# Scan sums in the tile of the turned squares, and the split of the probabilities inside the next keys' group

## Chip, core and metric

The kernel runs on one NeuronCore of a Trainium2 chip, as one launch. The metric is the device time of one execution in microseconds (us), smaller is better. Input and output lie in the chip's memory.

## What is computed

A decoder of two layers over 272 tokens (16 learned meta tokens and 256 tokens of input), width 2048, 16 heads of 128, all in float32. Layer one uses attention with a forget gate, layer two "stick-breaking" attention over keys and values made by `w_kv`. Each layer ends in an MLP of width 8192. The part that the change touches is the attention of layer two:

```python
def stick_breaking_attention(q, k, v):
    scale = HEAD_DIM ** -0.5
    outs = []
    for qs, qe in query_blocks(q.shape[1]):
        z = jnp.einsum('bqhd,bkhd->bhqk', q[:, qs:qe], k[:, :qe]).astype(jnp.float32) * scale
        q_pos = jnp.arange(qs, qe)
        k_pos = jnp.arange(qe)
        mask = k_pos[None, :] < q_pos[:, None]
        log_beta = jax.nn.log_sigmoid(z)
        log_one_minus = jnp.where(mask, jax.nn.log_sigmoid(-z), 0.0)
        suffix = lax.cumsum(log_one_minus, axis=3, reverse=True) - log_one_minus
        a = jnp.where(mask, jnp.exp(log_beta + suffix), 0.0).astype(v.dtype)
        outs.append(jnp.einsum('bhqk,bkhd->bqhd', a, v[:, :qe]))
    return jnp.concatenate(outs, axis=1)
```

The cumulative sum over the keys runs from the last key back; the kernel makes it with a scan.

## The kernel before

**Products.** Activations lie feature-major: 128 features on the partitions, tokens along the free axis. A large product is made by `gemm_group` (L215), which makes 512 output features (four accumulators, m = 0 to 3, of 128) from all 2048 inputs in 192 matmuls. To keep float32 accuracy, each operand is split into a rounded part (hi) and the rest (lo), and three products of parts are added. The weights come from memory in four blocks (kb = 0 to 3), each of two halves; `weights` (L186) loads a half into a tile `raw` (issued by SyncE), ScalarE rounds it to `whi` (L210), and VectorE subtracts to get `wlo` (L211). There are four buffers for halves, so a half can be split only when TensorE has used the one four places earlier. In blocks 0 and 3 the products run accumulator by accumulator over both halves, in blocks 1 and 2 half by half. So a half in the middle serves 24 products. There are four accumulators, and an accumulator is free for the next group when its result has been copied out (for keys and values L480, on VectorE).

**Layer two's attention** (L695 to L777) goes through four groups g of four heads. For each g there is a keys' group (a `gemm_group` with `w_kv[2g]`, L698) and a values' group (`w_kv[2g + 1]`, L743). Beside the values' group the other engines work on the heads in two pairs (pr = 0, 1), L712 to L734:

- the scores z are made on TensorE (L717, L718) and masked (L719); `softplus` (L688 to L693) gives e; a scan on VectorE (L723) gives the sums from the last key back; z minus the sums (L726), then an exponential on ScalarE (L727), gives the probabilities
- `turn_probabilities` (L446) transposes squares of 32 by 32 into a tile `raw` (L451, VectorE) and stores it with four DMAs to `p_dram` (L454, issued by ScalarE)
- `probabilities_back` (L456) reads them back turned, with two DMAs per pair (L461, ScalarE): 512 columns into `raw` and 256 into `p1`
- `split` (L368) rounds the 512 columns on ScalarE (L370) and subtracts on VectorE (L371). The result `p0` (both parts) and `p1` are the moving operands of `weighted` (L423) and L771

In the trace the turned tile and its read-back have the names raw_p, and the split's result the name p. After the values' group, `squares` (L386) turns the values in the same way (L394), `scratch` (L397) stores them with eight DMAs (L401), and `outputs1` (L754) reads them back (L406), splits them (v, L412) and makes the outputs. `outputs1` of group g is called inside the keys' group of g + 1, ahead of its last weight block; for the last group it is called directly.

**Order.** Engines take their instructions in order. DMAs are issued from ScalarE's queue and stand in it between its other instructions. The order of each queue is worked out when the kernel is built (`schedule_with_timeline_sim`, L911). `behind(ins, other)` (L171) adds an ordering without a wait: ins is placed no earlier than other. The list `issued` holds the matmuls of the current group, 0 to 191, so `issued[140]` as a place means behind the 141st product. Before the change the read-backs of the two pairs stand behind products 140 and 176 of the values' group, and both splits behind its last:

```python
        probabilities_back(pps, (140, 176))
        for pr in range(2):
            raw, p0, p1 = pps[pr]
            behind(split(p0.rearrange("p x i q -> p x (i q)"), raw[:, :512]), issued[-1])
```

**Buffers.** Tiles of one tag share its buffers. The tag "pp" has three: for q2 (the split queries, L707 and L708), e, sums and raw of each pair, and turned (the transposed values). p0 of the first pair uses the one buffer of the tag "kT", p0 of the second one of four of "qT", p1 one of two of "relu".

Of the kernel before, what the change touches and what calls it, by code (L numbers as in the profile page):

```python
# [9 lines left out]
F32 = mybir.dt.float32  # L10
# [5 lines left out]
P = 128  # L16
# [17 lines left out]
def yoco_kernel(ctx: ExitStack, tc: tile.TileContext, hT_in, gains, b_f, w_f, w_qkv0, w_o0, w_up, w_dn,  # L34
# [10 lines left out]
    att = ctx.enter_context(tc.tile_pool(name="att", bufs=2))  # L45
# [117 lines left out]
    queued, pinned, issued = [], [False], []  # L163
# [7 lines left out]
    def behind(ins, other):  # L171
        tc.add_manual_dep(ins.ins, other.name, mybir.DependencyInfo(mybir.DependencyClass.NoSync,
                                                                    mybir.DependencyReason.DATA))
# [194 lines left out]
    def split(hl, src):  # L368

        on_act = nc.scalar.activation(hl[:, 0], src, AF.Copy)  # L370
        nc.vector.tensor_tensor(out=hl[:, 1], in0=src, in1=hl[:, 0].bitcast(F32), op=ALU.subtract)  # L371
        return on_act
# [44 lines left out]
    def by_parts(out, a, b, start, stop=False):  # L417

        for k, (i, j) in enumerate(((0, 0), (0, 1), (1, 0))):
            product = nc.tensor.matmul(out, a[i], b[j], start=start and k == 0, stop=stop and k == 2)  # L420
        return product
# [34 lines left out]
    def probabilities_back(pps, places):  # L456
        for pr, at in enumerate(places):
            raw, p0, p1 = pps[pr]
            back = p_dram[pr].rearrange("c j a (h x) -> (c j) (a h) x", h=2)
            for dst, src in ((raw[:, :512], back[:, :, :64]), (p1.rearrange("p i q -> p (i q)"), back[:, :, 64:])):  # L460
                behind(nc.scalar.dma_start(dst.rearrange("p (m x) -> p m x", m=8), src), issued[at])  # L461
# [8 lines left out]
    for g in range(4):  # L470
# [8 lines left out]
        def evac_kv(m, acc, t):  # L479
            nc.vector.tensor_tensor(out=t[:, m, :], in0=acc, in1=box["rstd"], op=ALU.mult)  # L480
# [61 lines left out]
        pps = []  # L542
        for pr in range(2):
            raw = att.tile([P, 2, 2, 256], F32, tag="pp", bufs=3, name=f"raw_p0_{g}_{pr}").rearrange("p x i q -> p (x i q)")
            p0 = att.tile([P, 2, 2, 256], F32R, tag="pp", bufs=3, name=f"p0_{g}_{pr}")
            p1 = tmp.tile([P, T], F32, tag="relu", name=f"p1_{g}_{pr}")[:, :2 * P].rearrange("p (i q) -> p i q", i=2)
# [34 lines left out]
        for pr in range(2):  # L581
            raw, p0, p1 = pps[pr]
# [100 lines left out]
    def backward(a):  # L683

        (step, n), = a.ap[1:]
        return bass.AP(a.tensor, a.offset + (n - 1) * step, [a.ap[0], (-step, n)])
# [9 lines left out]
    for g in range(4):  # L696
        kT = att.tile([P, 4, T], F32, tag="kT", bufs=1, name=f"kT1_{g}")
        gemm_group(w_kv[2 * g], xc, 0, lambda m, acc: evac_kv(m, acc, kT), {3: outputs1} if g else {})  # L698
        q = qT1[g]

        k0 = att.tile([P, 4, T], F32R, tag="vT", bufs=1, name=f"k0_{g}")
        k1 = ao.spare[:, 4 * g:4 * g + 4]
        for j in range(0, 4, 2):
            nc.scalar.activation(k0[:, j:j + 2], kT[:, j:j + 2], AF.Copy)
            nc.vector.tensor_tensor(out=k1[:, j:j + 2], in0=kT[:, j:j + 2], in1=k0[:, j:j + 2].bitcast(F32),
                                    op=ALU.subtract)
        q2 = att.tile([P, 2, 4, P], F32R, tag="pp", bufs=3, name=f"q12_{g}")  # L707
        split(q2, q[:, :, P:S])  # L708
        z = att.tile([P, 4, 416], F32, tag="s", bufs=1, name=f"z_{g}")

        pps = []
        for pr in range(2):  # L712
            zp = z[:, 2 * pr:2 * pr + 2]
            for i in range(2):
                j = 2 * pr + i
                ps = patt.tile([P, 512], F32, tag="patt", name=f"pz_{g}_{j}")
                product = by_parts(ps[:, 144:416], [q2[:, k, j, :] for k in range(2)], [k0[:, j], k1[:, j]], True, True)  # L717
                placed_behind(nc.tensor.matmul(ps[:, 0:144], q[:, j, 0:P], kT[:, j, :144], start=True, stop=True), product)  # L718
                nc.vector.tensor_tensor(out=z[:, j], in0=ps[:, :416], in1=maskB, op=ALU.add)  # L719
            e, sums = (att.tile([P, 2, 2, 256], F32, tag="pp", bufs=3, name=f"{x}_{g}_{pr}")  # L720
                       .rearrange("p x i q -> p (x i q)")[:, :832] for x in ("e", "sums"))
            softplus(e.rearrange("p (i k) -> p i k", i=2), zp)
            nc.vector.tensor_tensor_scan(out=sums, data0=goes_on.rearrange("p i k -> p (i k)"), data1=backward(e), initial=0.0,  # L723
                                         op0=ALU.mult, op1=ALU.add)
            zf = zp.rearrange("p i k -> p (i k)")
            nc.vector.tensor_tensor(out=zf, in0=zf, in1=backward(sums), op=ALU.subtract)  # L726
            nc.scalar.activation(zp, zp, AF.Exp)  # L727

            raw = att.tile([P, 2, 2, 256], F32, tag="pp", bufs=3, name=f"raw_p1_{g}_{pr}").rearrange("p x i q -> p (x i q)")
            p0 = att.tile([P, 4, T], F32R, tag=("kT", "qT")[pr], bufs=(1, 4)[pr], name=f"p01_{g}_{pr}")  # L730
            p0 = p0.rearrange("p h t -> p (h t)")[:, :1024].rearrange("p (x i q) -> p x i q", x=2, i=2)
            p1 = tmp.tile([P, T], F32, tag="relu", name=f"p11_{g}_{pr}")[:, :2 * P].rearrange("p (i q) -> p i q", i=2)
            turn_probabilities(z, raw, pr)
            pps.append((raw, p0, p1))  # L734

        pm = patt.tile([P, 512], F32, tag="patt", name=f"pm1_{g}")
        placed_behind(nc.tensor.transpose(pm[:, 0:P], corners(z[:, :, P:144], z[:, :, 400:416], f"sm1_{g}"), ident), product)
        pm_sb = att.tile([P, 192], F32, tag="pm_sb", bufs=1, name=f"pm_sb1_{g}")
        nc.vector.tensor_tensor(out=pm_sb[:, :P].rearrange("p (b q) -> p b q", q=M), in1=maskD, op=ALU.mult,
                                in0=pm[:, P - M:P].unsqueeze(1).to_broadcast([P, 8, M]))  # L740

        vT = att.tile([P, 4, T], F32, tag="vT", bufs=1, name=f"vT1_{g}")
        gemm_group(w_kv[2 * g + 1], xc, 0, lambda m, acc: evac_kv(m, acc, vT))  # L743
        probabilities_back(pps, (140, 176))
        for pr in range(2):
            raw, p0, p1 = pps[pr]
            behind(split(p0.rearrange("p x i q -> p x (i q)"), raw[:, :512]), issued[-1])


        turned = squares(vT, "pp", f"1_{g}") if g < 3 else None  # L750
        if g < 3:
            scratch(turned, issued[-2:])

        def outputs1(g=g, vT=vT, pps=pps, pm_sb=pm_sb, turned=turned):  # L754
            if turned is not None:
                vs = values_back(turned, issued[64:80:8], issued[112:128:8], f"1_{g}")
            pv = patt.tile([P, 512], F32, tag="patt", name=f"pvc_{g}")
            nc.tensor.transpose(pv[:, :P], corners(vT[:, :, P:144], vT[:, :, 256:T], f"vc1_{g}"), ident)
            vc_sb = att.tile([P, P], F32, tag="vm_sb", bufs=1, name=f"vc_sb_{g}")
            nc.scalar.copy(vc_sb, pv[:, :P])  # L760
            own = att.tile([P, 8, M], F32, tag="own", bufs=1, name=f"own1_{g}")
            for pr in range(2):
                v0, v1 = vs[pr] if turned is not None else token_major(vT, pr, 0, f"1_{g}_{pr}")
                po = patt.tile([P, 2, 256], F32, tag="patt", name=f"po1_{g}_{pr}")
                p0, p1 = in_order(*pps[pr][1:])
                for i in range(2):
                    product = weighted(po, v0, p0, i)
                    if pr == i == 0:
                        placed_behind(nc.tensor.matmul(pv[:, P:2 * P], vc_sb, pm_sb[:, :P], start=True, stop=True), product)
                        nc.scalar.copy(own, pv[:, P:2 * P].rearrange("p (c q) -> p c q", c=8))  # L770
                    nc.tensor.matmul(po[:, i, P:], v1[:, i, :], p1[:, i], start=False, stop=i == 1)  # L771
                ends = po.rearrange("p i (c q) -> p (i c) q", c=2)[:, :, P - M:]
                nc.vector.tensor_tensor(out=ends, in0=ends, in1=own[:, 4 * pr:4 * pr + 4], op=ALU.add)
                put_split(ao, 4 * g + 2 * pr, 2, M, S, po)

        if g == 3:
            outputs1()  # L777
# [141 lines left out]
```

## Time and profile before

| | |
|---|---|
| median of 3 runs | 2306.78 us (2300.99, 2306.78, 2307.44) |
| the profiled execution | 2299.98 us |
| its span, first to last instruction | 2298.2 us |
| mean granted TensorE clock | 0.996 of full speed |
| busy: TensorE, VectorE, ScalarE, GpSimd | 2270.4, 1343.1, 1057.8, 37.9 us |
| memory traffic | 186 GB/s over the span |
| layer two's attention with its keys and values | about 1260 to 1518 us of the span |

How to read the profile: PE is TensorE, PEld its weight loads, DVE VectorE, ACT ScalarE, POOL GpSimd, SP SyncE; "ACTq" marks what ScalarE's sequencer does itself, here DMA issues. L370 is line 370 of the kernel. A row of a timeline has the start in us from the span's start, the duration in us, engine, line, operation, "result<-operands", the shape and the count of merged instructions; a bracket at the end gives the idle time just before and the instruction that ended it. A row of waits has the total in us, the number of waits and the longest. A row of stretches has the stretch and its length, the busy us and counts of PE, PEld, DVE, ACT and POOL, and then the granted clock, the DMA engines' busy share and GB/s. A row of the chain has start, duration, engine, and what ran with how many instructions.

### The profile page before, as it was taken

Reading aid. Unit: us, or ns where it says so; the run is one execution under the profiler, and the core shown is the slowest. Engines: PE = TensorE matmul, PEld = TensorE weight load, DVE = VectorE, ACT = ScalarE, POOL = GpSimd, SP = SyncE. Lnnn points to the kernel's source line nnn. Section 1 sums busy time; section 2 is a strip of 40 time slices with the busy share of each in tenths; the row PEclk is TensorE's granted clock in tenths of the full one; section 3 lists DMA queues with packets and bytes.
Section 4 is the critical chain, followed back from the end, with each engine's and each line's share of the span. In section 5 each row is a group of like instructions: output and inputs, shape, how many; then the busy total and the mean of one; then the engine's idle time right before and its main releaser. Section 6 shows DMA issues by size and latency. Waiting matters only on the chain.

```text
span 2298.2 us, 44896 instructions
## 1 busy us (share of the span) xinstructions
PE 2270.4 (99%) x18830; PEld 2259.3 (98%) x18830; DVE 1343.1 (58%) x1943; ACT 1057.8 (46%) x1451; POOL 37.9 (2%) x78
## 2 busy tenths in 40 slices
PE   9999999999999999999999999999999999999998
PEld 9999999999999999999999989899999999999998
DVE  7766666554554455455566666666555555555555
ACT  6444454453343344344454444455543543543554
POOL 0000000000000000000000000000000000000001
PEclk9999999999999999999999999999999999999999
DMA  7766665555555555555555566656566566565564
GB/s 242 227 196 193 216 183 174 184 174 183 168 187 179 171 187 175 182 168 187 179 178 191 173 180 193 183 184 202 185 192 202 184 201 196 190 201 185 189 205 138
DMA packets 167418, 431.46 MB, mean 188 GB/s; under 512 B 48800, under 2 KB 65072, under 8 KB 167216
## 3 DMA queue, kind: packets, MB, share of 16 engines
q1 hardware_dynamic: 113760, 406.29, 54.8%
q10 hardware_dynamic: 53456, 22.31, 3.9%
q8 instruction: 147, 2.41, 0.4%
q14 instruction: 55, 0.45, 0.1%
HBM read 416.99 MB, written 11.55 MB: 186 GB/s over the span
## 4 chain that ended last, share of the span: by engine, by line
PE 92%; DMA 3%; DVE 2%; issue 1%; ACTq 1%; ACT 1%; POOL 0%; SPq 0%; POOLq 0%; DVEq 0%
PE acc L177 90%; DMA p_dram<-raw_p 1%; DMA raw_p<-p_dram 1%; DVE wlo L211 1%; PE po L420 0%; ACT whi L210 0%; ACTq L454 0%; DMA p<-p_dram 0%; DVE sums L723 0%; DVE z L726 0%; PE ps L420 0%; PE pz L420 0%; DMA v_dram<-turned 0%; DVE raw_p L451 0%; ACTq L461 0%
## 5 line engine op out<-in xcount | busy, mean ns | idle before, releaser
L211 DVE TENSOR_TENSOR wlo<-raw,whi 128x1024 fp32r<-128x1024 f32 (+1 forms) x773 | 927.3, 1216 | 694.6 <-ACT whi L210 687.7
L210 ACT ACTIVATE whi<-raw 128x1024 fp32r<-128x1024 f32 (+1 forms) x773 | 796.0, 1050 | 941.1 <-PE acc L177 895.0
L177 PE MATMUL acc<-x_m,whi 128*128 128x272 f32 (+1 forms) x4096 | 643.0, 281 | 0.0
L177 PE MATMUL acc<-x_u,whi 128*128 128x272 f32 (+1 forms) x3968 | 626.0, 281 | 0.0
L177 PEld LDWEIGHTS acc<-x_m,whi 128*128 128x128 f32 x4096 | 565.8, 188 | 0.1
L177 PEld LDWEIGHTS acc<-x_u,whi 128*128 128x128 f32 x3968 | 550.3, 188 | 0.0
L177 PE MATMUL acc<-x_m,wlo 128*128 128x272 f32 (+1 forms) x2048 | 440.7, 281 | 0.0
L177 PE MATMUL acc<-x_u,wlo 128*128 128x272 f32 (+1 forms) x1984 | 431.5, 281 | 0.0
L177 PE MATMUL acc<-x_a,whi 128*128 128x272 f32 (+1 forms) x2048 | 354.9, 286 | 0.2 <-ACT whi L210 0.2
L177 PEld LDWEIGHTS acc<-x_m,wlo 128*128 128x128 f32 x2048 | 323.3, 188 | 0.0
L177 PEld LDWEIGHTS acc<-x_u,wlo 128*128 128x128 f32 x1984 | 315.1, 188 | 0.0
L177 PEld LDWEIGHTS acc<-x_a,whi 128*128 128x128 f32 x2048 | 300.8, 188 | 1.5 <-ACT whi L210 0.5
L177 PE MATMUL acc<-x_a,wlo 128*128 128x272 f32 (+1 forms) x1024 | 253.5, 285 | 0.0
L177 PE MATMUL acc<-x_kv,whi 128*128 128x272 f32 x1024 | 199.0, 293 | 12.3 <-ACT whi L210 8.8
L177 PEld LDWEIGHTS acc<-x_kv,whi 128*128 128x128 f32 x1024 | 164.6, 193 | 13.7 <-ACT whi L210 9.5
L177 PEld LDWEIGHTS acc<-x_a,wlo 128*128 128x128 f32 x1024 | 175.5, 188 | 0.8 <-DVE ssq_a L143 0.4
L177 PE MATMUL acc<-x_o,whi 128*128 128x272 f32 (+1 forms) x1024 | 163.0, 282 | 1.4 <-DVE vT L480 1.4
L177 PE MATMUL acc<-x_kv,wlo 128*128 128x272 f32 x512 | 150.0, 293 | 1.9 <-DVE wlo L211 1.9
L177 PEld LDWEIGHTS acc<-x_o,whi 128*128 128x128 f32 x1024 | 142.2, 188 | 1.6 <-DVE vT L480 1.6
L292 DVE TENSOR_TENSOR hT<-acc,hT 128x272 f32<-128x272 f32 (+1 forms) x156 | 67.3, 432 | 75.5 <-PE acc L177 75.3
L177 PE MATMUL acc<-x_o,wlo 128*128 128x272 f32 (+1 forms) x512 | 110.8, 282 | 0.0
L177 PEld LDWEIGHTS acc<-x_kv,wlo 128*128 128x128 f32 x512 | 99.1, 194 | 2.7 <-DVE wlo L211 2.7
(220 smaller groups left out, 1045.3 us busy)
## 6 DMA issues: line engine op xcount, KB each, us to landing
raw<-w_up SPq DMA_DIRECT2D x256, 512.0 KB, 4.1
raw<-w_dn SPq DMA_DIRECT2D x256, 512.0 KB, 3.9
raw<-w_qkv SPq DMA_DIRECT2D x92, 512.0 KB, 4.2
raw<-w_o SPq DMA_DIRECT2D x64, 512.0 KB, 4.3
raw<-w_kv SPq DMA_DIRECT2D x64, 512.0 KB, 4.5
raw<-w_q SPq DMA_DIRECT2D x32, 512.0 KB, 4.3
p_dram<-raw_p ACTq DMA_DIRECT2D x64, 96.0 KB, 4.5
raw_p<-p_dram ACTq DMA_DIRECT2D x16, 256.0 KB, 5.4
```

The lines of the kernel that those rows point to most:

```text
L177: ins = nc.tensor.matmul(*args, **kw).ins
L210: on_act = nc.scalar.activation(hp, src, AF.Copy)
L211: on_dve = nc.vector.tensor_tensor(out=lp, in0=src, in1=hp.bitcast(F32), op=ALU.subtract)
L292: nc.vector.tensor_tensor(out=hT[:, c, t0:], in0=acc, in1=hT[:, c, t0:], op=ALU.add)
```

## The change

The sums of a pair's scan get no tile of their own; they are written into the tile `raw`, which later holds the turned probabilities, and which is therefore taken ahead of the scan. The split of the probabilities leaves the end of the values' group. It now stands at the head of `outputs1` and, for the first three groups of heads, is placed behind products 36 (first pair) and 72 (second pair) of the next keys' group; for the last group of heads it stays behind the last product. The second pair's read-back is placed behind product 184 instead of 176.

```diff
-            e, sums = (att.tile([P, 2, 2, 256], F32, tag="pp", bufs=3, name=f"{x}_{g}_{pr}")
-                       .rearrange("p x i q -> p (x i q)")[:, :832] for x in ("e", "sums"))
+            e, raw = (att.tile([P, 2, 2, 256], F32, tag="pp", bufs=3, name=f"{x}_{g}_{pr}")
+                      .rearrange("p x i q -> p (x i q)") for x in ("e", "raw_p1"))
+            e, sums = e[:, :832], raw[:, :832]
...
-            raw = att.tile([P, 2, 2, 256], F32, tag="pp", bufs=3, name=f"raw_p1_{g}_{pr}").rearrange("p x i q -> p (x i q)")
...
-        probabilities_back(pps, (140, 176))
-        for pr in range(2):
-            raw, p0, p1 = pps[pr]
-            behind(split(p0.rearrange("p x i q -> p x (i q)"), raw[:, :512]), issued[-1])
-
-
+        probabilities_back(pps, (140, 184))
...
         def outputs1(g=g, vT=vT, pps=pps, pm_sb=pm_sb, turned=turned):
+            for pr in range(2):
+                raw, p0, p1 = pps[pr]
+                behind(split(p0.rearrange("p x i q -> p x (i q)"), raw[:, :512]), issued[(36, 72)[pr] if g < 3 else -1])
             if turned is not None:
```

## The prediction

> **What bounds the kernel now.** I read the page first: span, busy time, chain.
>
> ```profile
> span 2298.2 us, 44896 instructions
> PE 92%; DMA 3%; DVE 2%; issue 1%; ACTq 1%; ACT 1%; POOL 0%; SPq 0%; POOLq 0%; DVEq 0%
> ```
>
> TensorE sets the time: it is 92% of the chain that ended last, so only what lets TensorE wait less, or run at a better clock, is worth anything. The profiled execution took 2299.98 us; the runs shown have a median of 2306.78. I make the sum against the first and move the result to the second at the end.
>
> The diff touches the second layer's attention alone. So the next view is the waits of TensorE from 1280 to 1525 us (engine, line, who is waited for; us in total, times, longest).
>
> ```profile
> PE acc L177 <- ACT whi L210: 8.8, 3, 3.2
> PE acc L177 <- DVE vT L480: 4.9, 4, 1.7
> PE po L420 <- ACT p L370: 2.4, 1, 2.4
> PE pm L737 <- POOL pk_sm L438: 2.1, 4, 1.1
> PE acc L177 <- DVE wlo L211: 1.9, 3, 0.7
> ```
>
> Some 20 us in all. What happens three times happens between one group of four heads and the next (from 0 to 1, 1 to 2, 2 to 3). Here is TensorE's timeline at the first of these; the bracket is idle time and who ended it.
>
> ```profile
> 1315.03 0.53 PE L177 MATMUL acc<-x_kv,whi 128*128 128x272 f32 x2 [1.09 <-DVE vT L480]
> 1331.39 0.52 PE L177 MATMUL acc<-x_kv,whi 128*128 128x272 f32 x2 [3.23 <-ACT whi L210]
> 1332.65 0.42 PE L177 MATMUL acc<-x_kv,wlo 128*128 128x272 f32 x1 [0.74 <-DVE wlo L211]
> ```
>
> Why these waits? ScalarE's timeline of the same stretch (ACTq rows are DMA issues, which stand in the same queue) and VectorE's:
>
> ```profile
> 1307.49 0.54 ACTq L461 DMA_DIRECT2D raw_p<-p_dram  x1
> 1313.27 0.63 ACT L370 ACTIVATE p<-raw_p 128x512 fp32r<-128x512 f32 x1 [6.83 <-DMA raw_p<-p_dram]
> 1313.81 1.99 ACT L210 ACTIVATE whi<-raw 128x1024 fp32r<-128x1024 f32 x2
> 1315.94 0.90 ACT L727 ACTIVATE z<-z 128x832 f32<-128x832 f32 x1
> 1317.50 1.06 ACT L210 ACTIVATE whi<-raw 128x1024 fp32r<-128x1024 f32 x1
> 1319.78 2.05 ACTq L454 DMA_DIRECT2D p_dram<-raw_p  x4
> 1324.78 0.53 ACTq L461 DMA_DIRECT2D raw_p<-p_dram  x1
> 1326.06 2.80 ACTq L401 DMA_DIRECT2D v_dram<-turned  x3
> 1329.38 0.63 ACT L370 ACTIVATE p<-raw_p 128x512 fp32r<-128x512 f32 x1 [10.82 <-DMA raw_p<-p_dram]
> 1330.28 1.06 ACT L210 ACTIVATE whi<-raw 128x1024 fp32r<-128x1024 f32 x1 [0.27 <-ACT p L370]
> ```
>
> ```profile
> 1308.30 1.89 DVE L723 TENSOR_TENSOR_SCAN sums<-goes_on,e 128x832 f32<-128x832 f32 x1
> 1313.93 0.69 DVE L371 TENSOR_TENSOR p<-raw_p,p 128x512 fp32r<-128x512 f32 x1 [3.41 <-ACT p L370]
> 1314.54 0.43 DVE L480 TENSOR_TENSOR vT<-acc,rstd_a 128x272 f32<-128x272 f32 x1
> 1314.89 1.01 DVE L726 TENSOR_TENSOR z<-z,sums 128x832 f32<-128x832 f32 x1
> 1316.17 2.39 DVE L211 TENSOR_TENSOR wlo<-raw,whi 128x1024 fp32r<-128x1024 f32 x2
> 1318.49 1.26 DVE L451 STREAM_TRANSPOSE raw_p<-z 128x128 f32<-128x128 f32 x6
> ```
>
> Two things are to be seen. First, the split of the first pair's probabilities (L370 at 1313.27) stands in the queue until its read-back lands, and VectorE's half (L371) with it. Behind it wait the copy of the values (L480), for which TensorE waits 1.09, and the second pair's z (L726). Second, from 1319.78 to 1330.28 ScalarE makes no weight half: 10.5 us of stores, of waiting for them, of read-backs and the stores of v. I call this the **block**. TensorE runs dry inside it. Only the end of it is the second split.
>
> The gap is not all. The chain's rows (start, us, products) show 30 products after each gap, and 24 at the usual pace; the table of stretches shows the granted clock (the number after POOL's).
>
> ```profile
> 1332.65 5.53 PE acc L177 x30
> 1396.29 6.18 PE acc L177 x30
> 1454.63 5.54 PE acc L177 x30
> 1342.71 2.97 PE acc L177 x24
> ```
>
> ```profile
> 1331.39:1338.00 6.61, 5.87 (x32) 5.65 (x33) 5.28 (x6) 5.06 (x9) 0.00 (x0) 0.74 0.85 283
> 1395.03:1402.00 6.97, 6.53 (x30) 6.21 (x31) 5.28 (x6) 4.17 (x8) 0.00 (x0) 0.56 0.80 234
> 1515.01:1521.00 5.99, 5.81 (x47) 5.61 (x48) 5.07 (x7) 3.21 (x5) 0.00 (x0) 1.00 0.59 180
> ```
>
> Usual pace is 2.97/24 = 0.124 us a product, 3.71 for 30. So the slow stretches lose 1.82 + 2.47 + 1.83 = 6.1 us. The last row follows the 2.4 us wait of the list (PE po): there the clock stayed at 1.00. So gaps of 2.4 cost nothing beside themselves, and the three near 3 do.
>
> **The change part by part.**
>
> *Scan sums in raw's tile.* No instruction comes or goes; of the eight tiles that a group of heads takes from the tag "pp" two go. The transposes (L451) overwrite the sums after L726 has read them, both on VectorE and with L727 between them, so no new wait: 0. It makes room: both raw tiles and turned now live into the next keys' group and fill the tag's three buffers. The split of the next queries (L708) needs such a buffer and moves behind the first probability split.
>
> *The splits move behind products 36 and 72 of the next keys' group* (of 192; for the last group of heads they stay at the end). Per transition two ScalarE instructions of 0.63 and two of 0.69 on VectorE move, and the queries' split, of the same size. They issue no DMA. Cover: weight halves cost 1.06 on ScalarE and one is needed per 24 products, 2.97 us, so ScalarE has the room, outside the block. If that cover were gone it would be 3 x 0.63 = 1.9 us per transition.
>
> *What the first move frees.* The keys' group starts at 1310.9: 24 products (2.97) before the stall that began at 1315.03 - 1.09 = 1313.9. The scan ends at 1310.19; without the split, two copies (0.43 each) and L726 (1.01) end at about 1312.0 and L727 at about 1313.1. Then two wlo (2.39) and the transposes (1.26) end near 1315.9, where now they end at 1319.75: 3.8 us sooner. The copy of the values is then in time: three of the four waits on vT go (4.9 x 3/4 = 3.7) and, as L727 feeds the corners, three of the four on pk_sm (2.1 x 3/4 = 1.6). **Minus 5.3.** The fourth is the last group's, whose code hardly moves.
>
> *What is late next: the block.* Its head cannot move by the whole 3.8 if, as now, the weight half at 1317.50 goes first. That half needs a buffer which product 42 frees: 1310.9 + 42 x 0.124 = 1316.1, done at 1317.2. So the block starts at 1317.2 instead of 1319.78 and ends 2.6 sooner, and 0.6 more as the split at its end is gone: the weight half at 1327.1, TensorE at work 1.1 later, at 1328.2. TensorE, without its earlier stalls, needs it after 120 products and two transposes: 1310.9 + 14.9 + 0.2 = 1326.0. A gap of 2.2 stays. The second transition starts its block later, behind two weight halves, and has the longer block:
>
> ```profile
> 1379.00 2.01 ACT L210 ACTIVATE whi<-raw 128x1024 fp32r<-128x1024 f32 x2
> 1381.29 1.89 ACTq L454 DMA_DIRECT2D p_dram<-raw_p  x4
> 1388.33 5.03 ACTq L401 DMA_DIRECT2D v_dram<-turned  x5
> 1393.94 1.04 ACT L210 ACTIVATE whi<-raw 128x1024 fp32r<-128x1024 f32 x1
> ```
>
> Here the split waited not for its data but behind five v stores of 5.03 us; the block is 12.65. Its two halves come behind a wait on vT too and start about 5.3/3 = 1.8 sooner, the block ends 1.8 + 0.6 = 2.4 sooner, and TensorE asks 1.8 sooner: of a gap of 8.8/3 = 2.9, about 2.3 stay. I take 2.2 for each: 8.8 - 6.6 = **minus 2.2**, bounds 0 and 8.8. The wlo waits (1.9) I leave.
>
> *Clock.* A gap of 2.2 lies beside the 2.4 that cost nothing, not beside those near 3: **minus 6.1**. The bounds are 0 and 6.1.
>
> The Trainium skill, "TensorE: Matmul & The Clock Gate", Part 1 (the HAM clock gate), says that the array falls to half clock after an idle window of about 3.4 us and needs about as long at work to come back. The trace disagrees on the size: idle times of at most 3.23 us were followed by a mean clock of 0.56 and 0.74. An estimate by that page, half of 3.4 us lost three times, would be 5.1 in place of 6.1, and the sum 1 us smaller.
>
> *A new wait.* The values' split needs the v read-back, which follows the block.
>
> ```profile
> 1335.92 0.76 DVE L371 TENSOR_TENSOR v<-turned,v 128x256 fp32r<-128x256 f32 x2
> 1338.02 0.40 PE L420 MATMUL po<-p,v 128*128 128x256 f32 x2
> ```
>
> There are 1.3 us between them. TensorE comes earlier by (5.3 + 2.2 + 6.1)/3 = 4.5 per transition, the block, and v with it, by 2.5 to 3.2, so v would be up to 4.5 - 2.5 - 1.3 = 0.7 late. I take 0.5: **plus 1.5**, bounds 0 and 2.1.
>
> *Read-back of the second pair behind product 184 instead of 176.* Eight products, 1.0 us, but it waits for the store to land anyway (1324.78): 0, at most 1.0 each.
>
> Sum: -5.3 - 2.2 - 6.1 + 1.5 = **-12.1**. That is 2287.9 against the profiled execution and 2294.7 against the median; I give 2294.
>
> **The rivals.**
>
> *All gaps close* (15%). If both weight halves go ahead of a block of 10 us, it starts at 1316.1 + 2.0 and ends at 1328.1, when the half after these is needed only at 1310.9 + 144 x 0.124 + 0.2 = 1329.0. For: the second transition has this order now. Against: its block is 12.65, and the stores become ready sooner, not later. Saved: 5.3 + 8.8 + 1.9 + 6.1 = 22: 2285.
>
> *The block moves ahead of the weight half that now precedes it* (27%). The order of ScalarE's queue is worked out when the kernel is built (L911), and the page of before cannot show the new one. For: the transposes are done at 1315.9, before product 42 at 1316.1, so the stores could go first. Against: by 0.2 us only, and the order shown has the half first. Then the block ends at 1315.9 + 9.9 = 1325.8, weights are usable 2.4 later (as from 1330.28 to 1332.65), at 1328.2, but 96 products remain instead of 72, 2.97 us. Gain 4.45 - 2.97 = 1.5 per transition, the clock drop stays: -4.5, 2302. This is also the case in which the change does what it says, and the wait merely changes its place.
>
> *Slower: the same, with a long block* (13%). If the block is as in the second transition, 12.65, weights are usable at 1315.9 + 12.65 + 2.4 = 1331.0 with 96 products left: 1.3 later than now, and the gap, from product 96 (1322.9) on, is some 7 us, so that the clock drop is at least the largest seen, 2.47, 0.6 more than the others. That is 1.9; for a gap twice as long as any shown I take 2.7 each: +8, 2315. It decides at a block of 11.4 us. For: one v store of the five took long beside the read-backs. Against: the first transition's block has 10.5 with the split in it.
>
> **How the numbers follow.** Forecast 45%, all gaps closed 15%, block ahead 27%, slower 13%. A measurement of this kernel can tell about 0.3% from no change, 7 us. Faster: the forecast (its edge, with the clock drop staying, is -6, so nearly all of it) and the second: 0.56. Same: block ahead, and the forecast's edge: 0.31. Slower: 0.13. The forecast alone reaches from 2284 to 2302. The range reaches from 2279 (the closed gaps against the profiled execution, 2278) to 2309, block ahead with a little lost, and leaves out most of the slower case.
>
> **What would show it.** Right: no idle time on vT between groups of heads; L726 directly behind the scan and the copies; no ScalarE wait for raw_p in the values' group; TensorE's gap on whi about 2.2 and the clock at 1.00 behind it. Wrong: the gap on whi one weight half earlier and longer than 4 us (block ahead), waits of TensorE on v or p in the last quarter of the keys' group, or gaps of 2.2 with the clock at 0.7 behind them.

## The result, and the profile after

| | before | after |
|---|---|---|
| median | 2304.62 us (9 runs, 2300.99 to 2308.91) | 2299.23 us (9 runs, 2297.45 to 2301.88) |
| the profiled execution, span | 2299.98, 2298.2 us | 2298.19, 2296.5 us |
| mean granted TensorE clock | 0.996 | 0.995 |

After to before is 0.9975, 95% interval [0.9965, 0.9985]: 5.4 us less, a quarter of a per cent. The interval excludes 1, but the gain is smaller than the 0.3% which the prediction called the least that can be told, and less than half of the 12.1 us that it forecast. The page of after, span and chain:

```profile
span 2296.5 us, 44901 instructions
PE 94%; DVE 2%; DMA 2%; issue 1%; ACTq 1%; ACT 0%; POOL 0%; POOLq 0%; SPq 0%; DVEq 0%
```

TensorE's waits in after, in the same stretch from 1280 to 1525 us (total, times, longest):

```profile
PE acc L177 <- ACT whi L210: 14.3, 3, 5.8
PE pvc L756 <- POOL pk_vc L438: 2.7, 1, 2.7
PE acc L177 <- DVE wlo L211: 1.6, 3, 0.7
```

The waits on vT, pm and p are gone. The three on whi grew from 8.8 to 14.3, and a new one came in the last group, on the small copies by GpSimd that L756 reads (pk_vc). Of 20 us, 18.6 are left. TensorE's timeline in after, at the first, second and third transition:

```profile
1323.64 0.82 PE L177 MATMUL acc<-x_kv,whi 128*128 128x272 f32 x2 [5.81 <-ACT whi L210]
...
1383.81 0.82 PE L177 MATMUL acc<-x_kv,whi 128*128 128x272 f32 x2 [4.55 <-ACT whi L210]
...
1444.00 0.52 PE L177 MATMUL acc<-x_kv,whi 128*128 128x272 f32 x2 [3.99 <-ACT whi L210]
```

In before TensorE ran dry after 120 products of the keys' group (144 at the second transition). Here it does after 48, each time, when the first weight block is used up: the whole second weight block (kb = 1) is late. ScalarE's queue in after shows why:

```profile
1306.79 0.88 ACT L728 ACTIVATE z<-z 128x832 f32<-128x832 f32 x1
1308.92 0.54 ACTq L461 DMA_DIRECT2D raw_p<-p_dram  x1
1309.50 0.68 ACTq L461 DMA_DIRECT2D p<-p_dram  x1
1310.33 6.32 ACTq L454 DMA_DIRECT2D p_dram<-raw_p  x4
1316.75 2.39 ACTq L401 DMA_DIRECT2D v_dram<-turned  x5
1319.26 0.53 ACTq L461 DMA_DIRECT2D raw_p<-p_dram  x1
1319.82 0.68 ACTq L461 DMA_DIRECT2D p<-p_dram  x1
1320.53 1.90 ACTq L401 DMA_DIRECT2D v_dram<-turned  x3
1322.53 1.06 ACT L210 ACTIVATE whi<-raw 128x1024 fp32r<-128x1024 f32 x1 [14.86 <-DMA raw_p<-p_dram]
```

From 1308.92 on stand 16 DMA issues, with no split among them. Counted as the prediction counts it, from the second pair's stores to the next weight half, the block has 12.2 us (1310.33 to 1322.53) against 10.5. It starts 9.5 us sooner, but all of it stands ahead of the second weight block's halves. And the four stores of the second pair (L454), which took 2.05 us to issue in before, take 6.32. They follow the first pair's read-back directly. ScalarE no longer waits for the read-back at a split; it sits about as long (6.83 and 6.32 us) in the issue of the next stores.

Why the block starts so early is seen at e and the transposes. First before (e of the second pair, ScalarE), then after (e on ScalarE; the scan and the second transposes on VectorE):

```profile
1300.36 0.88 ACT L690 ACTIVATE e<-z 128x832 f32<-128x832 f32 x1
```

```profile
1295.01 0.88 ACT L690 ACTIVATE e<-z 128x832 f32<-128x832 f32 x1
...
1303.56 1.88 DVE L724 TENSOR_TENSOR_SCAN raw_p<-goes_on,e 128x832 f32<-128x832 f32 x1
...
1309.03 1.27 DVE L451 STREAM_TRANSPOSE raw_p<-z 128x128 f32<-128x128 f32 x6
```

The second pair's chain begins 5.4 us sooner and its transposes come 9.5 us sooner (1318.49 in before), where the prediction had 3.8. The built programs show which buffer of "pp" each tile gets. In before the first pair's raw takes the one that q2 leaves, so the second e takes that of the first e, which is free only after the first pair's scan, and it stands in ScalarE's queue behind the first pair's exponential (L727). In after raw has a buffer already, the one with the sums, and the second e takes the one that q2 leaves. The clock behind the three gaps (table of stretches, after):

```profile
1323.64:1331.00 7.36, 6.92 (x38) 6.60 (x39) 6.27 (x7) 5.54 (x9) 0.00 (x0) 0.67 0.87 263
1383.81:1391.00 7.19, 6.75 (x32) 6.43 (x33) 5.81 (x6) 4.79 (x7) 0.00 (x0) 0.57 0.88 259
1444.00:1451.00 7.00, 6.25 (x27) 6.04 (x28) 5.81 (x6) 4.56 (x7) 0.00 (x0) 0.54 0.86 252
```

The drop stays. At the first transition the end of the keys' group, counted at full clock, is 1331.39 + 72 x 0.124 = 1340.3 in before and 1323.64 + 144 x 0.124 = 1341.5 in after. So nothing was gained there, even without the slower clock. From the first scores of group 0 to those of group 3 before took 182.15 us and after 182.92; from there to the first sum of squares ahead of the MLP (L148), 133.3 and 130.0. In these two executions (1.8 us apart, the medians 5.4) the gain lies in the last group, which has no v stores and no next keys' group.

### The profile page after: what moved, and what is told of

Its sections match the earlier page's. It is cut to its first block, busy times and chain, and to the rows that moved or that the text cites. A ratio compares the mean times of both kernels' runs of the same rounds, so it can differ in the third digit from the quotient of the medians.

```text
span 2296.5 us, 44901 instructions
## 1 busy us (share of the span) xinstructions
PE 2269.9 (99%) x18830; PEld 2260.0 (98%) x18830; DVE 1344.9 (59%) x1943; ACT 1058.7 (46%) x1451; POOL 36.7 (2%) x78
## 4 chain that ended last, share of the span: by engine, by line
PE 94%; DVE 2%; DMA 2%; issue 1%; ACTq 1%; ACT 0%; POOL 0%; POOLq 0%; SPq 0%; DVEq 0%
PE acc L177 91%; DMA raw_p<-p_dram 1%; DVE wlo L211 1%; DMA raw<-w_qkv 1%; PE po L420 0%; DVE raw_p L724 0%; DMA p_dram<-raw_p 0%; ACT whi L210 0%; ACTq L454 0%; DVE raw_p L451 0%; ACTq L401 0%; PE pz L420 0%; PE ps L420 0%; DVE z L727 0%; DVE e L693 0%
## 5 line engine op out<-in xcount | busy, mean ns | idle before, releaser
L177 PE MATMUL acc<-x_kv,whi 128*128 128x272 f32 x1024 | 199.5, 294 | 14.3 <-ACT whi L210 14.3
```

The source lines that it names most:

```text
L177: ins = nc.tensor.matmul(*args, **kw).ins
```

## The experiments

Each kernel was timed beside the kernel before. The theory after the result: sharing the tile is what brings the second pair forward, and the DMA issues in ScalarE's queue are what gives the gain back. The rival: sharing is neutral, as predicted, and moving the splits explains it all. Theory and rival are told apart first by doing one part alone.

Each difference in the table has an interval of some 3 us to either side.

| median less that of before, us | neither part | sharing only | split moved only | both |
|---|---|---|---|---|
| v stores issued by ScalarE | 0 | -13.6 | -7.9 | -5.4 (after) |
| v stores issued by SyncE | -11.4 | -25.3 | -18.5 | -29.8 |

**Sharing alone.** The diff's first two hunks; the splits stay behind the values' group and the read-back at 176.

> Only the first part of the change: the sums in raw's tile; the splits stay behind the values' group and the second read-back behind product 176. Queue theory (the time follows from where the block of DMA issues stands in ScalarE's queue, and how long it is): sharing frees a buffer, so the second pair's softplus comes some 5 us sooner, as in the changed kernel; the first split still waits about 6 us for its read-back ahead of the second pair's stores; a block without weight halves still ends late. Time -3 to +3 us against before. Rival (the moved splits are what eats the gain, sharing is neutral): nothing moves, the second exponential stays about 10 us behind the first, and time is that of before. Second rival (sharing alone makes the 5 us): -5 us.

Measured: 2290.77, ratio 0.9939 [0.9926, 0.9953]. The theory and both rivals missed; the second transposes came at 1309.26 (after: 1309.03), so it is the sharing that brings them forward. The part that had been priced at 0 is worth 13.6 us, more than the whole change. TensorE's waits and ScalarE's queue in this kernel:

```profile
PE acc L177 <- ACT whi L210: 4.4, 3, 1.9
PE acc L177 <- DVE vT L480: 4.2, 3, 2.0
```

```profile
1314.92 0.63 ACT L370 ACTIVATE p<-raw_p 128x512 fp32r<-128x512 f32 x1 [7.16 <-DMA raw_p<-p_dram]
1314.92 1.78 ACTq L454 DMA_DIRECT2D p_dram<-raw_p  x4
1316.81 1.06 ACT L210 ACTIVATE whi<-raw 128x1024 fp32r<-128x1024 f32 x1 [1.25 <-DVE turned L394]
```

Here the split waits 7.16 us for the read-back, as in before. But the stores behind it issue in 1.78 us, and the weight halves of the second weight block follow at once: the first ahead of the v stores, the second (1317.77) after two of them. So it seems that the old wait held the stores back until they could go through quickly.

**The moved splits alone.** The other hunks; the sums keep their own tile.

> Only the second part: splits behind products 36 and 72 of the next keys' group and the read-back behind 184, sums in a tile of their own. Queue theory: the second pair comes as late as in before, so its stores go after the second block's weight halves; the waits on vT go, the gap lies ahead of the third block (product 96) and is 3 to 5 us; -3 to -9 us against before, level with the changed kernel or better. Rival (the moved splits delay the weight halves of the keys' group): as slow as the changed kernel, with weight halves queued behind the splits. Second rival (sharing makes the 5 us): 0.

Measured: 2296.42, 0.9969 [0.9956, 0.9981], as the theory expected: the two parts alone make 21.5 us, together 5.4. They undo each other. TensorE's wait on whi, the second pair's transposes, and ScalarE's queue:

```profile
PE acc L177 <- ACT whi L210: 11.8, 3, 6.4
```

```profile
1314.70 1.26 DVE L451 STREAM_TRANSPOSE raw_p<-z 128x128 f32<-128x128 f32 x6
1315.99 1.85 ACTq L454 DMA_DIRECT2D p_dram<-raw_p  x4
...
1322.10 2.89 ACTq L401 DMA_DIRECT2D v_dram<-turned  x5
1325.09 1.06 ACT L210 ACTIVATE whi<-raw 128x1024 fp32r<-128x1024 f32 x1 [10.89 <-DMA v_dram<-turned]
```

The transposes end at 1315.96, which is what the prediction worked out for the moved splits (1315.9, 3.8 us sooner than in before). The stores, issued in 1.85 us, and the v stores stand ahead of the weight half, and the gap stands at product 96 in all three transitions. This is the prediction's rival of the block ahead of the weight half, without the sharing.

**The v stores later.** The kernel after, with the v stores behind the next second block's weight halves.

```diff
-        if g < 3:
-            scratch(turned, issued[-2:])
+        stores = {1: lambda turned=turned: scratch(turned, issued[-2:])} if g < 3 else {}
...
-        gemm_group(w_kv[2 * g], xc, 0, lambda m, acc: evac_kv(m, acc, kT), {3: outputs1} if g else {})
+        gemm_group(w_kv[2 * g], xc, 0, lambda m, acc: evac_kv(m, acc, kT), {3: outputs1} if g else {}, stores)
```

> The changed kernel, but the eight v stores are placed behind the weight halves of the next keys' group's second block. Queue theory: the two halves go ahead of the v stores, the gap at product 48 of 4 to 6 us closes to 0 to 1, some of it comes back at product 96 (0 to 2 us) as the eight stores and the second read-back follow; no clock drop. -9 to -14 us against before, so -4 to -9 against the changed kernel. Rival (moved splits): no better than the changed kernel.

Measured: 2290.06, 0.9938 [0.9926, 0.9951], 14.3 us less than before, at the edge of what was expected. The gaps at product 48 are closed, but 1.97, 2.09 and 2.74 us on whi are left at product 96, where 0 to 2 were expected, and the granted clock behind the first of them is 0.75, where no drop was. The v stores ahead of the weight halves cost after some 9 us.

**The v stores in another queue.** The kernel after, the v stores of layer two issued by SyncE.

```diff
-    def scratch(t, products):
+    def scratch(t, products, queue=nc.scalar):
...
-                ins = nc.scalar.dma_start(v_dram[pr].rearrange("c j a x -> a j c x")[a], y[32 * a:32 * a + 32])
+                ins = queue.dma_start(v_dram[pr].rearrange("c j a x -> a j c x")[a], y[32 * a:32 * a + 32])
...
-            scratch(turned, issued[-2:])
+            scratch(turned, issued[-2:], nc.sync)
```

> The changed kernel, but the eight v stores of layer two are issued by SyncE instead of ScalarE. Queue theory: ScalarE's block loses some 4 us and the weight halves of the second block go behind the first four stores; gaps at the transitions under 1 us, -12 to -20 us against before, unless SyncE's weight loads come late behind stores that wait for VectorE: then TensorE waits on whi and whi on raw. Rival (moved splits): no better than the changed kernel.

Measured: 2274.52, 0.9871 [0.9858, 0.9885], 29.8 us less than before: better than expected, and the fastest of all kernels here. ScalarE and SyncE in it:

```profile
1310.00 5.67 ACTq L454 DMA_DIRECT2D p_dram<-raw_p  x4
1315.77 2.01 ACT L210 ACTIVATE whi<-raw 128x1024 fp32r<-128x1024 f32 x2 [9.17 <-DMA p_dram<-raw_p]
```

```profile
1314.66 3.73 SPq L401 DMA_DIRECT2D v_dram<-turned  x8
```

The four stores still take 5.67 us, but the weight halves come 6.8 us sooner than in after, in time. No wait on whi is left in TensorE's list:

```profile
PE pvc L756 <- POOL pk_vc L438: 3.2, 1, 3.2
PE acc L177 <- DVE wlo L211: 0.7, 1, 0.7
PE po L420 <- ACT v L370: 0.4, 1, 0.4
```

So eight issues per transition in the wrong queue cost after about 24 us. The Trainium skill, "DMA: Bandwidth & Descriptors", section "Issuing engines are not separate DMA queues", says that issuing from several engines saves only the issuing sequencer's time, usually small beside the DMA itself. The trace agrees that the issues take time of the sequencer, 2.39 + 1.90 us per transition on ScalarE in after, but with weight halves behind them that TensorE waits for, the gain wasn't small.

**The read-back behind the stores.** The kernel after, the first pair's read-back placed behind the second pair's stores.

```diff
+                back_in = nc.scalar.dma_start(dst.rearrange("p (m x) -> p m x", m=8), src)
+                behind(back_in, issued[at])
+                if stored is not None and pr == 0:
+                    behind(back_in, stored.ins)
```

> The changed kernel, but the first pair's read-back is placed behind the second pair's stores in ScalarE's queue; nothing else moves. Theory (a store issued behind a read-back in the same queue cannot be issued until that has drained, which is how the wait that left the split came back): the four stores take 2 us instead of the 4.4 to 6.3 of the changed kernel, TensorE's gap at product 48 falls from 4 to 6 us to 2 to 4, and the time by 3 to 9 us against the changed kernel. Rival (the issue is slow because the DMA engines are busy with weights as well): the stores still take 4 us or more and the time is that of the changed kernel.

Measured: 2295.98, 0.9968 [0.9956, 0.998], some 3 us less than after; the two intervals overlap, so this gain is not clear. ScalarE:

```profile
1310.04 2.04 ACTq L454 DMA_DIRECT2D p_dram<-raw_p  x4
...
1317.48 3.88 ACTq L401 DMA_DIRECT2D v_dram<-turned  x7
1321.46 1.06 ACT L210 ACTIVATE whi<-raw 128x1024 fp32r<-128x1024 f32 x1 [14.18 <-DMA v_dram<-turned]
```

Half right. The stores issue in 2.04 us, so it was the read-back ahead of them. But now a v store behind the read-back took 2.13 alone, the block ends at 1321.4 and gaps of 5.0, 3.8 and 4.5 us stay; 2 to 4 were expected. The wait changed its place once more.

**The v stores on SyncE, with one part or none.** Three kernels: sharing alone, the moved splits alone and before, each with the v stores of layer two issued by SyncE as in the diff above.

> Sums in raw's tile, splits in their old place, v stores issued by SyncE. With both parts of the change and the v stores on SyncE the kernel was 30 us faster than before; this tells what the moved splits add to that. Theory (with a short block the move is worth what was forecast for it, the wait on vT): ScalarE waits some 6 us for the read-back again, TensorE 1 to 2 us per transition on vT, and it is 4 to 8 us slower than with the move, -22 to -26 against before. Rival (the move is of no use at all): -30.

Measured: 2278.41, 0.9893 [0.988, 0.9906]. As expected: with the block short, the moved splits are worth 4.5 us on top of sharing (after with SyncE: 29.8). They take away the waits on vT, 3.8 us here.

> Splits moved, sums in a tile of their own, v stores issued by SyncE. It tells what sharing adds when the v stores are off ScalarE. Theory: the second pair comes 5 to 9 us later than with sharing, but the block is short enough: gaps of 0 to 1 us, the last group 3 us slower: -22 to -28 against before. Rival (sharing is what carries the gain): -15 or less.

Measured: 2285.26, 0.9928 [0.9911, 0.9945], a miss by 3.5 us. Without sharing the second pair is late, and the values' read-back, which stands behind the pair's, is issued at 1324.74 (1320.08 with both parts). TensorE waits for v:

```profile
PE po L420 <- ACT v L370: 7.1, 4, 2.8
```

> The kernel before, with nothing changed but the queue of the eight v stores (SyncE instead of ScalarE). Theory (ScalarE's block is what TensorE waits for in before as well): the gaps of 3 us on whi close, the waits on vT (5 us in all) stay: -10 to -18 against before. Rival (the splits' waits for their read-back are what made the gaps): the gaps stay, 0 to -4.

Measured: 2292.31, 0.9959 [0.9947, 0.9971]; the time is as expected, though the twelve runs spread from 2289.2 to 2301.5. No wait on whi is left in TensorE's list, so the v stores in ScalarE's queue already cost the kernel before some 11 us. But of the 5 us on vT only 2.9 stay, and 7.4 us on v are new: again part of the wait moved.

**The first pair's read-back on SyncE.** The kernel after with `nc.sync.dma_start` for the two DMAs of that pair in layer two.

> The kernel after, with the read-back of the first pair's probabilities issued by SyncE instead of ScalarE; everything else, the second pair's read-back and the eight v stores too, stays in ScalarE's queue. Theory (a store that stands behind the read-back in the same queue is taken slowly): the second pair's four stores issue in about 2 us (1.8 to 2.1) instead of 4.4 to 6.3, the block loses that and the 1.2 us of the two read-back issues, some 4 to 5 us; the gap on whi falls from 4.0 to 5.8 us to 0 to 2 and the clock stays up: 10 to 17 us faster than before. Rival (the read-back's packets load the DMA engines, whatever queue they come from): the stores still take 4 us or more to issue, only the 1.2 us go, gaps of 3 to 4.6 stay: 5 to 9 us faster than before. Second rival: SyncE waits for the first pair's stores to land, weight loads behind it come late and ScalarE waits for raw: no gain over the kernel after, or a loss.

Measured: 2300.81, 0.9986 [0.9977, 0.9994]: no faster than after, the time of the second rival. Its reason is another, though. ScalarE, the second pair's stores, the first v store and the fourth:

```profile
1309.63 1.92 ACTq L454 DMA_DIRECT2D p_dram<-raw_p  x4
```

```profile
1312.04 0.31 ACTq L401 DMA_DIRECT2D v_dram<-turned  x1
```

```profile
1318.52 0.31 ACTq L401 DMA_DIRECT2D v_dram<-turned  x1
```

The stores go in 1.92 us: it is the read-back in the same queue that slows them, as the theory had it. But the fourth v store, whose data are ready by 1312.5 (the last transpose of v), is issued at 1318.52. The built program tells why. In it every DMA, from SyncE's or ScalarE's queue, counts its landing on one of eight counters, taken in turn, and before it is issued waits for the DMA that used the counter last:

```
counter   3  4          5  6              7 0 1 2               3  4  5  6  7
DMA       read-back     weight halves     stores of the         stores
          of pair 1     of block kb = 2   second pair           of v
queue     SyncE         SyncE             ScalarE               ScalarE
```

So the third and fourth v store, on ScalarE, wait for two weight loads of SyncE. The issue of the second load on SyncE, and its time from issue to landing (last number):

```profile
1310.77 0.44 SPq L199 DMA_DIRECT2D raw<-w_kv  x1
```

```profile
raw<-w_kv SPq DMA_DIRECT2D x2, 512.0 KB, 7.7
```

1310.77 + 7.7 = 1318.5, which is when the store goes. At the third transition, in the same kernel:

```profile
1433.76 0.45 SPq L199 DMA_DIRECT2D raw<-w_kv  x1
```

```profile
raw<-w_kv SPq DMA_DIRECT2D x1, 512.0 KB, 6.9
```

```profile
1440.69 0.80 ACTq L401 DMA_DIRECT2D v_dram<-turned  x2
```

1433.76 + 6.9 = 1440.66. The times fit; no run took the counters away, so this cause is read from program and trace, not tried by itself. So the block ends at about the same time in three orders of it, for different reasons (next weight half 1322.53 in after, 1321.46 with the read-back later, 1322.46 here).

**Read-backs and v stores on SyncE.**

> The kernel after, with the v stores and both pairs' read-backs of layer two issued by SyncE. ScalarE keeps only the eight probability stores per group of heads. Theory: the weight halves already come in time with the v stores alone gone from ScalarE's queue, so at most the 3.9 us of TensorE waits that are left there can go: 28 to 34 us faster than before, about the same as with the v stores alone on SyncE. Rival (SyncE's queue becomes the bound: its waits for stores delay the weight loads behind them): 10 to 25 us faster, with TensorE or ScalarE waiting for weight loads.

Measured: 2280.1, 0.9895 [0.9882, 0.9907], 24.5 us less than before: the rival's number, some 5 us worse than with the v stores alone on SyncE. But TensorE doesn't wait for weights, as the rival had it; it waits for v, 4.5 us in four waits. The profiled executions of the two kernels lie only 1.0 us apart, so where the 5 us between the medians go isn't shown.

**Fewer v stores.** The kernel after, with a layout of the scratch in which one DMA stores a pair's v; the read-back takes four.

```diff
+                behind(nc.scalar.dma_start(v_whole[pr].rearrange("a j c x -> (a j) (c x)"), t[:, pr]), products[pr])
...
+                for c in range(4):
+                    dst = t[32 * c:32 * c + 32, pr].rearrange("j (a x) -> j a x", a=4)
+                    behind(nc.scalar.dma_start(dst, v_whole[pr][:, :, c, :].rearrange("a j x -> j a x")), read[pr])
```

> The kernel after, with the layout of the values' scratch in memory changed: per pair one store of 128 rows of 2 KB instead of four stores in 512-byte pieces, and four read-backs instead of one, all still issued by ScalarE. Two v stores instead of eight stand near the block, the second behind the second block's two weight halves, and the six more read-backs come after the weight halves. Theory (ScalarE's DMA issues ahead of the weight halves are the cost): the second pair's four stores still take 4 us or more to issue behind the read-back, but the weight halves come right behind them and one v store, some 5 us sooner than after; the gap on whi falls from 4.0 to 5.8 us to at most 1.5 and the clock stays up: 15 to 24 us faster than before. Rival (it is the bytes of the v stores in the queue, not the number of the issues): the gap stays above 3 us and the time within 3 us of the kernel after's. Second rival: the eight read-backs make v late: TensorE waits on v for 2 us or more per transition, 5 to 12 us faster than before.

Measured: 2278.15, 0.9891 [0.9876, 0.9907], 25.9 us less than before, a little more than expected. ScalarE:

```profile
1309.57 5.67 ACTq L463 DMA_DIRECT2D p_dram<-raw_p  x4
1315.33 0.40 ACTq L401 DMA_DIRECT2D v_whole<-turned  x1
1315.83 1.06 ACT L210 ACTIVATE whi<-raw 128x1024 fp32r<-128x1024 f32 x1 [9.06 <-DMA p_dram<-raw_p]
```

The slow stores stay, the weight half comes at 1315.83 instead of 1322.53, and the gap is gone: TensorE's list has no wait on whi. The store of 256 KB takes 0.40 us to issue, and each of 64 KB at this transition of after 0.40 to 0.46 (0.92 behind the second read-back). So the cost of an issue does not go by its bytes. What this kernel does not tell apart is the number of issues and their order: the second v store (1316.00) and the second pair's read-back (1316.94) now stand behind the first weight half too.

**Both: fewer v stores, and the first pair's read-back on SyncE.**

> The same layout of the values' scratch, and the first pair's read-back issued by SyncE too. Theory: with neither the slow issue behind the read-back nor v stores that wait for the weight loads of SyncE ahead of the weight halves, the second pair's stores issue in about 2 us, the weight halves come in time, no gap on whi above 0.5 us, the clock stays up: 22 to 30 us faster than before, 3 to 8 more than with the layout alone. Rival (SyncE's wait for the first pair's stores holds up the weight loads behind it): ScalarE waits for raw and TensorE on whi for 1 us or more per transition: 8 to 18 us faster than before.

Measured: 2285.86, 0.9927 [0.9911, 0.9942]: a miss, some 8 us slower than with the layout alone. The stores do issue in 1.84 us and TensorE has no wait on whi, as forecast; the rival's time is not far, but its reason isn't shown: ScalarE does idle 4.66 us ahead of the weight half at 1321.09, yet the second pair's read-back stands directly ahead of that half in the queue. It is issued only from 1319.74 to 1320.99 (from 1316.94 with the layout alone). The v read-backs stand behind it, and v comes late:

```profile
PE po L429 <- ACT v L371: 7.9, 6, 2.0
```

The read-back reads what the four stores write, so it needs them landed. Here the fourth is issued sooner, at 1312.49 instead of 1314.78, but takes longer from issue to landing (last number; this kernel, then the layout alone):

```profile
p_dram<-raw_p ACTq DMA_DIRECT2D x1, 96.0 KB, 7.1
```

```profile
p_dram<-raw_p ACTq DMA_DIRECT2D x1, 96.0 KB, 2.0
```

1312.49 + 7.1 = 1319.6 and 1314.78 + 2.0 = 1316.8: each read-back goes right after. It also counts on the counters of two weight halves (5 and 6), but these were free before: the second half landed at 1318.9 (1311.87 + 7.0). So the stores issue quickly, as the theory had it, but did not land sooner for it. Why they take longer to land isn't shown; the read-back and two weight halves are issued by SyncE at the same time (1309.73 to 1312.3).

## Why the prediction was right or wrong, point by point

The measured 2299.2 lies inside the range of 2279 to 2309, and the time fell, as forecast. But the mechanism was not the one forecast, so that the number lies in the range is luck. Two steps failed, the price of the sharing and the place of the block in ScalarE's queue. In the two profiled executions TensorE's waits in the attention fall by 1.7 us, from 20.3 (with 0.2 on VectorE's part of p) to 18.6, and the spans by the same: 9.9 us of waits go, and 8.2 come, 5.5 on whi and 2.7 on pk_vc.

- **vT and pk_sm, minus 5.3**: right. Neither is left in the list of waits of after. The wait on p of the last group (2.4) went too, and one on pk_vc (2.7) came for it.
- **Scan sums in raw's tile: 0**: this step failed first. The working looked for a new wait and for none that goes. It counted that two of eight tiles of the tag "pp" go, and priced that room only in the next keys' group, not for the second pair's e, which in before has to wait for the first e's buffer. Sharing alone measured 13.6 us. That the buffer does it is read from the built programs and the order; a fourth buffer with separate tiles was not tried.
- **The block starts 2.6 sooner and a gap of 2.2 stays, minus 2.2**: this failed twice over. The working has the weight half go first, with 0.2 us between the two. With the splits moved alone the transposes came when it said, but the stores went first, and the waits on whi were 11.8 us, not 6.6. With the sharing the transposes came 9.5 us sooner, not 3.8, and the whole block stood ahead of the second weight block's halves. The block also grew, 12.2 us for 10.5, because the stores are issued behind the read-back (6.32 for 2.05). The gaps measured 5.8, 4.6 and 4.0: plus 5.5 where minus 2.2 stood.
- **Clock, minus 6.1**: failed as a consequence; 0.67, 0.57 and 0.54 behind the gaps. The rule under it failed too (last section).
- **v late, plus 1.5**: 0 in after, since TensorE came no sooner. The mechanism is there: with gaps closed (read-backs on SyncE too) TensorE waits 4.5 for v.
- **The splits cost nothing**: right; the kernel that only moves them gained, and TensorE waits nowhere for p.
- **Read-back at 184: 0**: not tried by itself.
- **The rivals.** What came is "the block moves ahead of the weight half that now precedes it", at 27%: 2302 forecast, 2299.2 measured. As it was worked out, it is the kernel with the splits moved alone: stores at 1315.99 for 1315.9, the gap at product 96; 7.9 us less were measured there for 4.5. In the whole change the block started 5.6 us sooner than that (1310.33), was longer (12.2 for 9.9), and the gap stood at product 48, so that its 2302 lies so near is in part luck too. The slower rival had the length nearly right (12.65), but not the early start.

## What to carry to other kernels

A tile that is no longer taken is not only room: look for who waits to take one, and how far its whole chain comes forward. A DMA issue is an instruction of the engine that issues it; when a wait is removed ahead of a run of issues, ask what then stands ahead of the work that TensorE needs next, and move the issues (another queue, fewer pieces, behind that work) rather than the wait. Two parts that gain alone can undo each other: here they nearly add up (11.4, 25.3, 18.5, 29.8) only when the v stores have left ScalarE's queue.

## What the runs showed of the hardware

- Four stores of 96 KB that start within 0.8 us of the end of a read-back's two issues (256 and 128 KB) in the same queue took 3.8 to 6.3 us to issue, in all twelve places of the four kernels that have this order. Elsewhere in layer two they took 1.8 to 2.8 us, with two exceptions of 3.1 and 3.6; with that read-back in SyncE's queue or behind the stores, the first transition had 1.84 to 2.07. What makes the issue slow isn't shown.
- Eight counters, which this program's DMAs on both queues take in turn, tied a store on ScalarE to a weight load on SyncE (1318.52 and 1440.69 above).
- The length of a gap alone did not decide on the granted clock behind it. Sharing alone, behind gaps of 1.44 and 1.86 us:

```profile
1384.12:1391.00 6.88, 6.13 (x47) 5.92 (x48) 5.29 (x6) 4.48 (x8) 0.00 (x0) 1.00 0.77 233
1441.29:1448.00 6.71, 5.97 (x26) 5.75 (x27) 5.28 (x6) 4.41 (x8) 0.00 (x0) 0.53 0.73 234
```

The first kept 1.00 and the second fell to 0.53, while 2.4 us in before kept 1.00. What else decides was not tried. So the prediction's rule, that gaps of 2.4 us cost nothing beside themselves, does not hold.
